# Attention sums through VectorE's 32x32 blocks, a few new places in the second sweep, and a Newton step by scalars

## The chip, the cores and the metric

The kernel runs on one core of one Trainium2 chip. The metric is the device time of one execution in microseconds (us); it is measured as the median of several runs. The kernel's text is a Python program that issues instructions to five engines, each with its own queue in program order: PE (TensorE, matrix products and transposes; PEld is its weight load), DVE (VectorE), ACT (ScalarE), POOL (GpSimd) and SP (SyncE, which here only starts DMAs). ACT's queue starts some DMAs too.

## The reference

One encoder layer over 2048 tokens of width 1024, in float32. The input projection feeds two groups of heads: four heads of bidirectional gated linear attention, and four heads of latent attention with a full softmax. Both pass a SiLU gate, are put side by side, go through one output projection, and end in a residual with LayerNorm:

```python
h = x @ w_in                                    # all projections at once
o_a = rms_norm(o_fwd + o_bwd, norm_g) * silu(gate_a)        # per head, scans over the sequence
...
s = q_nope . k_nope + q_rope . k_rope           # per head, 2048 x 2048
p = softmax(s, axis=-1)
o_b = (p @ v) * silu(gate_b)
...
m = concatenate([o_a, o_b]) @ w_out
t = alpha * x + m
y = (t - mean(t)) * rsqrt(var(t) + 1e-5) * g + b
```

The change touches three small parts of that: the sum that the softmax divides by, the order of work in one sweep, and the `rsqrt` of the last line.

## The kernel before

Products in float32 are made of three matmuls. Each operand is split into a rounded high part (`hi`, a copy by ACT, L364) and a low part (`lo`, a subtraction by DVE or POOL, L370), and `mm3` adds high x high (L418), high x low (L419) and low x high (L420).

**Stages.** A first sweep goes backwards over 16 chunks of 128 tokens (to about 370 us). A second sweep (`sweep_c`, L1145) goes over them in eight steps of two chunks, makes the queries and keys of both groups, and finishes the linear attention (to about 562 us). Then come 16 blocks of softmax attention, each one head and 512 queries, against all 2048 keys in eight pairs of 128 (to about 1125 us), and the output projection by chunks with LayerNorm (the tail).

**Second sweep.** Each chunk's work is a list of named steps (`kvx`, `sqO`, `rml`, ...). A table, `PLACE_C`, gives each step two numbers, for the even and the odd chunk of a pair: the time, in units of one step, at which it is issued. `PLACE_C_LAST` (L284) replaces it in the last step. All steps are sorted by these numbers into one list, and `in_order` ties every engine's instructions into that order, so the tables fix each queue. The steps that the change moves are: `kvx` (L1390, three DVE transposes in 32x32 blocks of the values' high and low part and of the rotary keys, of one chunk; `skv` stores both chunks' from SP's queue), `sqO` (L1507, the squares of the linear attention's output, ACT), and the norm of the compressed queries and keys: `rml` (L431 and L432, a logarithm and an exponential by ACT), `ssm` (L1348, DVE, mean squares), `rmd` (L437 to L440, DVE, the Newton step of that norm). Beside them in the queues stand `xh` (xch, high part of a chunk of x, ACT), `cqTh` and `cqTl` (cqT_h by ACT and cqT_l by DVE, the parts of the compressed queries that PE multiplies at pqr), `krsh` (krs, the keys' high part, ACT), and qrx, qrT (turned rotary queries).

**Attention.** `PLACE` (L82) works in the same way, in units of one pair of keys: eight units are a block, and a block's work is spread over the next two. For each pair, `scores` (L1599 to L1603) writes two PSUM banks, pS, of which there are two pairs; `copy` (L1608) takes them to SBUF by ACT; `smax` (L1621) keeps the running maximum by DVE, reading pS, and so frees it; later `sub` (L1645, DVE) subtracts the maximum, `exp` (L1649, ACT), `hi` and `lo` split the probabilities, `pv` multiplies them with the values. The sum of the probabilities is gathered in two accumulators, four pairs by DVE in PSUM (ap, L1672) and four by POOL in SBUF (acc). `tot` (L1695, L1696, DVE) adds them up to one tile of 128 keys x 512 queries. `tsum` (L1708) turns it by four PE transposes, 128x128 each, into PSUM (sx); `rcp` sums over the keys (L1714, DVE) and takes the reciprocal (L1715); `keep` (L1720, on ACT's DMA queue) stores 512 single values to DRAM. The last block's sum runs in the tail, and the last two blocks' reciprocals go a way of their own, through `turn` (L1726, a PE transpose of 128x4, rt) and `rows` (L1732).

**Tail.** Each chunk's projection (`product`) is followed by `finish` (L2015 to L2027): mean and variance, a pass over two halves of 128x512 with the gain (lng), `rsqrt` of the variance, a second pass (L2026, with lnb), and the store. `rsqrt` is a logarithm and an exponential by ACT (L431, L432) and one Newton step by DVE in `rsqrt_b` (L437 to L440); for `finish` its operands have one element per partition. ACT's, POOL's and SP's order is fixed in the tail; DVE's is left to the scheduler.

## Time and profile before

| | |
|---|---|
| median of 3 runs | 1267.62 us (1267.16 to 1270.45) |
| the profiled execution | 1266.33 us |
| span of its trace | 1264.5 us, granted clock 0.997 |
| instructions | 19632 |
| DMA | 165.61 MB, 131 GB/s on average |

Busy time by stage, us:

| stretch | stage | PE | PEld | DVE | ACT | POOL |
|---|---|---|---|---|---|---|
| 0 to 32 | start | 26.02 | 24.59 | 21.83 | 22.94 | 0.21 |
| 32 to 500 | sweeps | 465.72 | 439.35 | 259.50 | 221.54 | 173.12 |
| 500 to 560 | second sweep's end | 57.49 | 55.05 | 37.06 | 28.28 | 28.10 |
| 560 to 680 | attention begins | 117.80 | 99.29 | 94.14 | 86.17 | 68.01 |
| 1095 to 1130 | attention ends | 35.00 | 29.01 | 16.94 | 3.75 | 18.33 |

How to read what follows: a row of the busy table gives an engine, its busy us, its share of the span and its instructions. A row in order of time gives the start in us, the duration, the engine, the line (L1621 is line 1621 of the kernel), the operation, output<-inputs by the program's names, shapes, and in square brackets the idle time ahead of it with what ended it. A row of a group gives its count, its busy us and the mean ns of one.

### The profile page before, as it was taken

What the parts mean: (1) busy time and instruction counts of PE and PEld (TensorE: products, weight loads), DVE (VectorE), ACT (ScalarE), POOL (GpSimd) and SP (SyncE); (2) the same over time, 40 slices, a digit from 0 to 9 for tenths busy, and PEclk for the clock granted to TensorE, in tenths of its full rate; (3) what the DMA queues carried; (4) which work ended last, traced back from release to release, by engine and by line L of the source; (5) the groups of instructions that cost most, each with busy time, mean ns of one, the idle gap of its engine ahead of it and who ended that gap; (6) DMA issues with size and microseconds to landing.
All of it is one profiled execution on the core that took longest, in us unless ns stands there. A gap on an engine that the chain in (4) does not pass through costs nothing.

```text
span 1264.5 us, 19632 instructions
## 1 busy us (share of the span) xinstructions
PE 1242.3 (98%) x6890; PEld 1094.2 (87%) x6890; DVE 906.0 (72%) x1654; ACT 725.8 (57%) x1149; POOL 721.7 (57%) x443
## 2 busy tenths in 40 slices
PE   8999999999999999999999999999999999999997
PEld 7999999999899999988788888888888888887886
DVE  6635555554565666575988888888888888379998
ACT  7543443444664545445788888788888888411110
POOL 0132323223364555421798888889999999935441
PEclk9999999999999999999999999999999999999999
DMA  8224655556757788868422222202244120477773
GB/s 294 79 81 123 139 143 139 144 135 159 268 179 212 227 244 239 240 183 195 73 37 48 41 43 43 59 9 59 59 94 92 41 43 26 125 205 199 206 199 116
DMA packets 284338, 165.61 MB, mean 131 GB/s; under 512 B 185574, under 2 KB 241774, under 8 KB 284240
## 3 DMA queue, kind: packets, MB, share of 16 engines
q1 hardware_dynamic: 276176, 162.23, 48.2%
q0 software_dynamic: 672, 2.10, 0.4%
q8 instruction: 55, 0.90, 0.4%
q10 hardware_dynamic: 7392, 0.03, 0.3%
q14 instruction: 43, 0.35, 0.1%
HBM read 105.54 MB, written 58.75 MB: 130 GB/s over the span
## 4 chain that ended last, share of the span: by engine, by line
PE 86%; DVE 5%; DMA 3%; issue 2%; SPq 2%; ACT 1%; POOL 1%; DVEq 0%; POOLq 0%; ACTq 0%
PE pz L1266 7%; PE ipm L1335 5%; PE o L418 5%; PE o L419 5%; PE o L420 5%; PE pS L1599 4%; PE pS L1600 4%; PE pS L1602 4%; PE pS L1601 4%; PE pS L1603 4%; PE ipa L418 4%; PE ipa L420 4%; PE ipa L419 4%; PE ipg L420 2%; PE ipg L418 2%; PE ipg L419 2%
## 5 line engine op out<-in xcount | busy, mean ns | idle before, releaser
L370 POOL TENSOR_TENSOR pl<-s,ph 128x1024 fp32r<-128x1024 f32 x128 | 306.6, 2412 | 51.5 <-ACT ph L364 40.9
L1621 DVE TENSOR_TENSOR rm<-pS,rm 128x512 f32<-128x512 f32 x210 | 144.8, 690 | 36.3 <-ACT s L1608 30.7
L1608 ACT ACTIVATE s<-pS 128x1024 f32<-128x1024 f32 x128 | 131.3, 1025 | 60.4 <-PE pS L1603 50.0
L1645 DVE TENSOR_TENSOR s<-s,mb 128x1024 f32<-128x1024 f32 x128 | 151.2, 1213 | 8.9 <-PE mb L1639 8.8
L364 ACT ACTIVATE ph<-s 128x1024 fp32r<-128x1024 f32 x128 | 135.0, 1057 | 16.7 <-PE o L420 16.1
L1649 ACT ACTIVATE s<-s 128x1024 f32<-128x1024 f32 x128 | 131.4, 1049 | 9.4 <-DVE s L1645 9.3
L418 PE MATMUL ipa<-wah,xah 128*128 128x384 f32 (+1 forms) x384 | 128.8, 335 | 5.4 <-ACT wah L364 5.4
L419 PE MATMUL ipa<-wal,xah 128*128 128x384 f32 (+1 forms) x384 | 124.6, 324 | 0.0
L420 PE MATMUL ipa<-wah,xal 128*128 128x384 f32 (+1 forms) x384 | 124.4, 324 | 0.0
L1085 POOL TENSOR_TENSOR Sb<-Sb,Us 64x512 f32<-64x512 f32 x15 | 19.9, 1325 | 170.1 <-DVE Us L1077 161.0
L1599 PE MATMUL pS<-qh,kvT 128*128 128x512 f32 x256 | 102.4, 400 | 0.8 <-DVE rm L1621 0.4
L418 PE MATMUL o<-ph,vh 128*128 128x512 f32 x256 | 101.0, 395 | 0.0
L1600 PE MATMUL pS<-ql,kvT 128*128 128x512 f32 x256 | 99.9, 390 | 0.0
L1602 PE MATMUL pS<-rh,kvT 128*128 128x512 f32 x256 | 99.9, 390 | 0.0
L1601 PE MATMUL pS<-qh,kvT 128*128 128x512 f32 x256 | 99.8, 390 | 0.0
L1603 PE MATMUL pS<-rl,kvT 128*128 128x512 f32 x256 | 99.7, 390 | 0.0
L420 PE MATMUL o<-ph,vl 128*128 128x512 f32 x256 | 99.7, 389 | 0.0
L419 PE MATMUL o<-pl,vh 128*128 128x512 f32 x256 | 99.6, 389 | 0.0
L1672 DVE TENSOR_TENSOR ap<-ap,s 128x512 f32<-128x512 f32 x120 | 83.1, 693 | 2.7 <-ACT s L1649 0.8
L370 POOL TENSOR_TENSOR ol<-of,oh 128x512 fp32r<-128x512 f32 x32 | 43.7, 1365 | 67.8 <-ACT oh L364 62.5
L418 PEld LDWEIGHTS ipa<-wah,xah 128*128 128x128 f32 x384 | 73.1, 190 | 8.3 <-ACT wah L364 5.4
L419 PEld LDWEIGHTS ipa<-wal,xah 128*128 128x128 f32 x384 | 73.1, 190 | 1.0 <-DVE wal L370 0.5
(303 smaller groups left out, 3416.1 us busy)
## 6 DMA issues: line engine op xcount, KB each, us to landing
xcf<-xT_dram SPq DMA_DIRECT2D x16, 512.0 KB, 5.7
xr<-x_dram SPq DMA_DIRECT2D x16, 512.0 KB, 5.9
out_dram<-rr SPq DMA_DIRECT2D x32, 256.0 KB, 2.1
xaf<-xT_dram SPq DMA_DIRECT2D x14, 512.0 KB, 4.1
oib<-oi_s SPq DMA_DIRECT2D x16, 256.0 KB, 4.9
qdb<-qd_s SPq DMA_DIRECT2D x16, 256.0 KB, 3.7
SU<-su_s SPq DMA_DIRECT2D x16, 256.0 KB, 4.8
ub<-u_s SPq DMA_DIRECT2D x16, 256.0 KB, 4.5
```

Of the source, the lines that this page charges most:

```text
L364: return nc.scalar.activation(dst, src, AF.Copy).ins
L370: return e.tensor_tensor(dst, src, hi.bitcast(F32), ALU.subtract).ins
L418: mm(out, ah, bh, start=start, stop=False)
L419: mm(out, ah, bl, start=False, stop=False)
L420: mm(out, al, bh, start=False, stop=stop)
L1599: mm(ps[:, e], kh, qh, start=True, stop=False)
L1600: mm(ps[:, e], kh, ql, start=False, stop=False)
L1601: mm(ps[:, e], kl, qh, start=False, stop=False)
L1602: mm(ps[:, e], kr, rh, start=False, stop=False)
L1603: mm(ps[:, e], kr, rl, start=False, stop=True)
L1621: V.tensor_tensor(d["rm"], src[:, e], d["rm"], ALU.max)
L1645: V.tensor_tensor(s, s, d["mb"][:, None, :].to_broadcast([P, 2, QB]), ALU.subtract)
```

## The change

It has three parts.

1. **Attention sums.** For the first 14 blocks a new step `tpart` follows `tot`: DVE transposes acc within 32x32 blocks (128 x 512 to 128 x 512), so that each partition holds, in each of 16 groups of 32, the values of 32 keys for one query, and sums each group: s16, 128 x 16. `tsum` then is one PE transpose of s16 to 16 x 128, `rcp` sums its four key groups for 16 x 32 queries and takes the reciprocal of 16 x 32, and `keep` stores 16 rows of 32 values. `tsum` gets another place. The last two blocks keep the old way.
2. **Second sweep.** Six numbers in the tables change.
3. **Newton step.** `rsqrt_b` gets a form for operands of one element per partition: three tensor_scalar instructions in which y and u are scalars by pointer, where three tensor_tensor and one tensor_scalar were.

Line numbers of the changed kernel are 1 higher up to L434, 6 higher up to L1703 and 21 higher at the end.

```diff
@@ PLACE @@
-    tsum=12.04,
+    tpart=11.25,
+    tsum=12.44,
@@ PLACE_C @@
-    kvx=(1.12, 1.44),
+    kvx=(1.3, 1.44),
@@ PLACE_C @@
-    sqO=(0.272, 0.988),
+    sqO=(0.272, 0.94),
@@ PLACE_C_LAST @@
-    rml=(0.162, 0.878),
+    rml=(0.187, 0.878),
@@ PLACE_C_LAST @@
-    ssm=(0.103, 0.733),
-    rmd=(0.254, 1.022),
+    ssm=(0.1025, 0.733),
+    rmd=(0.29, 1.022),
@@ rsqrt_b @@
     def rsqrt_b(self, u, y, t, w, r):
         nc = self.nc
+        if u.shape[1] == 1:
+            nc.vector.tensor_scalar(t, y, u, y, ALU.mult, ALU.mult)
+            nc.vector.tensor_scalar(t, t, -0.5, 1.5, ALU.mult, ALU.add)
+            nc.vector.tensor_scalar(r, t, y, None, ALU.mult)
+            return r
         nc.vector.tensor_tensor(t, y, u, ALU.mult)
         nc.vector.tensor_tensor(w, t, y, ALU.mult)
         nc.vector.tensor_scalar(t, w, -0.5, 1.5, ALU.mult, ALU.add)
@@ attention @@
                 p, tag = other if i == nb - 1 else (pX, "x")
                 return p.tile(shape, F32, tag=tag, name=name)
+            def tpart(i):
+                d = stt[i]
+                V.transpose(d["as"][:, 1], d["as"][:, 0])
+                d["s16"] = bs.tile([P, QB // 32], F32, tag="s16", name=f"s16_{i}")
+                V.tensor_reduce(d["s16"], d["as"][:, 1].rearrange("p (b k) -> p b k", k=32), AX.X, ALU.add)
+
             def tsum(i):
                 d = stt[i]
+                if i < nb - 2:
+                    d["x"] = pX.tile([P, 4, P], F32, tag="x", name=f"sx{i}")[0:QB // 32, 0]
+                    nc.tensor.transpose(d["x"], d["s16"], self.ident)
+                    return
                 d["x"] = close(i, [P, 4, P], f"sx{i}", (pA, "ap"))
                 for e in range(4):
                     nc.tensor.transpose(d["x"][:, e], d["as"][:, 0, e * P:(e + 1) * P], self.ident)
@@ attention @@
             def rcp(i):
                 d = stt[i]
-                rc = bs.tile([P, 4], F32, tag="rc", name=f"rc{i}")
+                if i < nb - 2:
+                    rc = d["rc"] = bs.tile([QB // 32, 32], F32, tag="rc", name=f"rc{i}")
+                    V.tensor_reduce(rc, d["x"].rearrange("b (k q) -> b q k", k=4), AX.X, ALU.add)
+                    V.reciprocal(rc, rc)
+                    return
+                rc = bs.tile([P, 4], F32, tag="rc4", name=f"rc{i}")
                 V.tensor_reduce(rc, d["x"], AX.X, ALU.add)
                 V.reciprocal(rc, rc)
                 d["rc"] = rc
             def keep(i):
                 h, b = blocks[i]
-                Ac.dma_start(self.r_s[b][:, h].rearrange("o (e p) -> p (o e)", p=P), stt[i]["rc"])
+                Ac.dma_start(self.r_s[b][:, h].rearrange("o (e q) -> (o e) q", q=32), stt[i]["rc"])
             def turn(i):
@@ attention @@
             put(0.5, nc.sync.dma_start, wv, self.ins["wv"])
             put(8.6, wv_hi)
             put(9.9, self.lo, wv_l, wv, wv_h, "pool")
-            own = (("tot", tot), ("tsum", tsum), ("rcp", rcp), ("keep", keep), ("oh", oh), ("ol", ol), ("y", y), ("yc", yc))
-            own_late = tuple(e for e in own if e[1] is not keep)
+            own = (("tot", tot), ("tpart", tpart), ("tsum", tsum), ("rcp", rcp), ("keep", keep), ("oh", oh), ("ol", ol), ("y", y), ("yc", yc))
+            own_late = tuple(e for e in own if e[1] not in (keep, tpart))
             for i in range(nb):
                 for j in range(NP):
                     t = NP * i + j
```

**The order, first place: DVE in an attention block.** In the middle of the program, from the last addition of block 5's sums to its reciprocal. The numbers after the tags are those of the block (and of the pair): s6_3 is the scores of block 6, pair 3, rm7 block 7's running maximum, mb6 block 6's maximum, ap the accumulator of DVE, ofl the low part of an output. Before:

```order
L1696 TENSOR_TENSOR acc5_8824<-ap5_8690,acc5_8824 128x512
L1621 TENSOR_TENSOR rm7_8917<-pS7_1_8906,rm7_8917 128x512 x2
L1645 TENSOR_TENSOR s6_3_8717<-s6_3_8717,mb6_8893 128x1024
L1621 TENSOR_TENSOR rm7_8917<-pS7_2_8935,rm7_8917 128x512 x2
L1645 TENSOR_TENSOR s6_4_8767<-s6_4_8767,mb6_8893 128x1024
L1645 TENSOR_TENSOR s6_5_8796<-s6_5_8796,mb6_8893 128x1024
L370 TENSOR_TENSOR ofl5_8999<-o5_8756,ofh5_8989 128x512
L1621 TENSOR_TENSOR rm7_8917<-pS7_3_8971,rm7_8917 128x512 x2
L1672 TENSOR_TENSOR ap6_8968<-ap6_8968,s6_0_8624 128x512
L1714 TENSOR_REDUCE rc5_9042<-sx5_8982 128x4
L1715 RECIPROCAL rc5_9042<-rc5_9042 128x4
```

After, from the row behind that addition:

```order
L1627 TENSOR_TENSOR rm7_8917<-pS7_1_8906,rm7_8917 128x512 x2
L1712 STREAM_TRANSPOSE acc5_8824<-acc5_8824 128x512
L1714 TENSOR_REDUCE s16_5_8958<-acc5_8824 128x16
L1651 TENSOR_TENSOR s6_3_8717<-s6_3_8717,mb6_8893 128x1024
L1627 TENSOR_TENSOR rm7_8917<-pS7_2_8935,rm7_8917 128x512 x2
L1651 TENSOR_TENSOR s6_4_8767<-s6_4_8767,mb6_8893 128x1024
L1651 TENSOR_TENSOR s6_5_8796<-s6_5_8796,mb6_8893 128x1024
L371 TENSOR_TENSOR ofl5_8999<-o5_8756,ofh5_8987 128x512
L1627 TENSOR_TENSOR rm7_8917<-pS7_3_8974,rm7_8917 128x512 x2
L1678 TENSOR_TENSOR ap6_8971<-ap6_8971,s6_0_8624 128x512
L1731 TENSOR_REDUCE rc5_9042<-sx5_8991 16x32
L1732 RECIPROCAL rc5_9042<-rc5_9042 16x32
```

The transpose and the sum of acc5 stand ahead of the subtraction for pair 3 of block 6, so that three subtractions, ofl5 and two further pairs of maxima are issued behind them; the rows of rc5 keep their place with smaller shapes. On PE, `L1708 MATMUL sx5_8982<-ident_213,acc5_8824 128x128 x4` became `L1720 MATMUL sx5_8991<-ident_213,s16_5_8958 16x128`, between the same scores, pS7_3 and pS7_4.

**Second place: the second sweep's last step.** Chunks 12 and 14 on DVE, from the keys' turns to the low part of the queries. rm14 is the norm's scale of chunk 14 (ipm14 its input), kvx6 the turned keys and values, Ob14 and ss14 belong to the linear attention's norm. Before, with the third turn first:

```order
L1390 STREAM_TRANSPOSE kvx6_6656<-krs12_6414 128x128
L1446 STREAM_TRANSPOSE qrx12_6660<-qrf12_6542 128x256
L1540 TENSOR_TENSOR krf14_6662<-ipm14_6560,cos_257 128x64
L1544 TENSOR_TENSOR rope1_14_6663<-ipm14_6560,sin_258 128x32 x2
L1512 TENSOR_REDUCE Ob14_6595<-og14_6667 128x4
L1513 TENSOR_SCALAR ss14_6677<-Ob14_6595 128x4
L437 TENSOR_TENSOR rm14_t_6673<-ipm14_6560,ssm14_6637 128x2
L438 TENSOR_TENSOR ipm14_6560<-rm14_t_6673,ipm14_6560 128x2
L439 TENSOR_SCALAR rm14_t_6673<-ipm14_6560 128x2
L440 TENSOR_TENSOR rm14_r_6674<-rm14_t_6673,ipm14_6560 128x2
L370 TENSOR_TENSOR qrT6_6682<-qrx12_6660,qrT6_6682 128x256
L370 TENSOR_TENSOR cqT_l6_6485<-tm13_6669,cqT_h6_6484 128x2x128
```

After:

```order
L1452 STREAM_TRANSPOSE qrx12_6656<-qrf12_6542 128x256
L1546 TENSOR_TENSOR krf14_6658<-ipm14_6560,cos_257 128x64
L1550 TENSOR_TENSOR rope1_14_6659<-ipm14_6560,sin_258 128x32 x2
L1518 TENSOR_REDUCE Ob14_6595<-og14_6663 128x4
L1519 TENSOR_SCALAR ss14_6668<-Ob14_6595 128x4
L371 TENSOR_TENSOR qrT6_6678<-qrx12_6656,qrT6_6678 128x256
L371 TENSOR_TENSOR cqT_l6_6485<-tm13_6665,cqT_h6_6484 128x2x128
L443 TENSOR_TENSOR rm14_t_6674<-ipm14_6560,ssm14_6637 128x2
L444 TENSOR_TENSOR ipm14_6560<-rm14_t_6674,ipm14_6560 128x2
L445 TENSOR_SCALAR rm14_t_6674<-ipm14_6560 128x2
L446 TENSOR_TENSOR rm14_r_6675<-rm14_t_6674,ipm14_6560 128x2
L1396 STREAM_TRANSPOSE kvx6_6696<-vh_3893 128x128
```

The four rows of rm14 and the three turns moved behind qrT6 and cqT_l6. On ACT at the same place (rm14_l is the logarithm, the second ipm14 row the exponential of the norm) before:

```order
L1342 ACTIVATE sqm14_6636,ssm14_6637<-ipm14_6560 128x256
L1343 ACTIVATE sqm14_6636,ssm14_6637<-ipm14_6560 128x128
L1507 ACTIVATE og14_6667<-Ob14_6595 128x512
L431 ACTIVATE rm14_l_6672<-ssm14_6637 128x2
L432 ACTIVATE ipm14_6560<-rm14_l_6672 128x2
L364 ACTIVATE cqT_h6_6484<-tm13_6669 128x2x128
L364 ACTIVATE qrT6_6682<-qrx12_6660 128x256
L364 ACTIVATE vh_3893<-ckv13_6634 128x128
```

After:

```order
L1348 ACTIVATE sqm14_6636,ssm14_6637<-ipm14_6560 128x256
L1349 ACTIVATE sqm14_6636,ssm14_6637<-ipm14_6560 128x128
L1513 ACTIVATE og14_6663<-Ob14_6595 128x512
L365 ACTIVATE cqT_h6_6484<-tm13_6665 128x2x128
L432 ACTIVATE rm14_l_6673<-ssm14_6637 128x2
L433 ACTIVATE ipm14_6560<-rm14_l_6673 128x2
L365 ACTIVATE qrT6_6678<-qrx12_6656 128x256
L365 ACTIVATE vh_3893<-ckv13_6634 128x128
```

cqT_h6 moved ahead of rm14_l and the exponential. In the steady steps ACT's order xch, krs, og became og, xch, krs, and the even chunk's turns stand later on DVE.

**Third place: the tail.** DVE at chunk 5's LayerNorm; u5 is the variance, ln5_y the result of ACT's exponential, rr5 the chunk. Before:

```order
L2023 SCALAR_TENSOR_TENSOR rr5_12192<-rr5_12192,mv5_12198,lng_11712 128x512 x2
L437 TENSOR_TENSOR ln5_t_12205<-ln5_y_12207,u5_12199 128x1
L438 TENSOR_TENSOR ln5_t_12205<-ln5_t_12205,ln5_y_12207 128x1
L439 TENSOR_SCALAR ln5_t_12205<-ln5_t_12205 128x1
L440 TENSOR_TENSOR ln5_r_12206<-ln5_t_12205,ln5_y_12207 128x1
L2026 SCALAR_TENSOR_TENSOR rr5_12192<-rr5_12192,ln5_r_12206,lnb_11713 128x512 x2
```

After:

```order
L2044 SCALAR_TENSOR_TENSOR rr5_12187<-rr5_12187,mv5_12193,lng_11712 128x512 x2
L439 TENSOR_SCALAR ln5_t_12200<-ln5_y_12202,u5_12194 128x1
L440 TENSOR_SCALAR ln5_t_12200<-ln5_t_12200 128x1
L441 TENSOR_SCALAR ln5_r_12201<-ln5_t_12200,ln5_y_12202 128x1
L2047 SCALAR_TENSOR_TENSOR rr5_12187<-rr5_12187,ln5_r_12201,lnb_11713 128x512 x2
```

The place is the same; four instructions became three, of another operation.

## Prediction

> **What bounds the kernel now.** I read the page's busy shares first, then the busy time by stage, then the order of time at the places that the change touches, and last who waited for whom. The page, and of the stages the steady part of attention and the output tail (columns: stretch, its length, then busy us and instructions of PE, PEld, DVE, ACT, POOL, then granted clock, DMA share, GB/s):

> ```profile
> PE 1242.3 (98%) x6890; PEld 1094.2 (87%) x6890; DVE 906.0 (72%) x1654; ACT 725.8 (57%) x1149; POOL 721.7 (57%) x443
> ...
> 680.00:1095.00 415.00, 415.00 (x1906) 343.19 (x1905) 352.31 (x469) 343.58 (x371) 376.94 (x165) 1.00 0.25 54
> ...
> 1130.00:1264.50 134.50, 125.24 (x574) 103.76 (x573) 124.18 (x198) 19.49 (x53) 57.00 (x42) 0.98 0.64 186
> ```

> In attention PE never rests: 415.00 of 415 us. Whatever leaves PE's queue there comes off the span, as long as nobody else becomes late; DVE is at 85% and POOL at 91%. In the tail PE and DVE are both nearly full (125 and 124 of 134.5), so a gain of DVE counts only where PE waits for it.

> **Attention: PE.** For 14 of the 16 blocks four transposes per block become one. PE's sums, a lone transpose of 4 columns (the last two blocks' reciprocals), and the place in one block:

> ```profile
> L1708 PE MATMUL sx<-ident,acc x64: 270/272/273, 639.9 to 1122.7; 128*128 128x128 f32 x64
> ...
> L1726 PE MATMUL rt<-ident,rc x2: 271/272/272, 1144.6 to 1170.3; 128*4 128x128 f32 x2
> ...
> 764.43 0.60 PE L1708 MATMUL sx<-ident,acc 128*128 128x128 f32 x4
> 764.79 0.48 PE L1599 MATMUL pS<-qh,kvT 128*128 128x512 f32 x1
> ```

> Four take 0.60 us and one alone 0.272, so each after the first costs (0.60 - 0.272)/3 = 0.109 us. The lone 4-column transpose also takes 0.272, so I take the new one with 16 columns as one of the old: three times 0.109 are saved, 0.33 us a block, 14 x 0.33 = **4.6 us**. The ends: 0 if another engine takes the time back, 4.6 if none does.

> **Attention: DVE.** It gets a transpose of 128x512 and a sum of 128x512 in SBUF, and its old sum of 128x512 out of PSUM becomes one over 16x128, the reciprocal one over 16x32. Neither new form stands in this trace at this place; the nearest rows (of oT and og in the second sweep, the old sum and reciprocal, and a 128x128 operation out of PSUM):

> ```profile
> L1529 DVE STREAM_TRANSPOSE oT<-og 128x512 f32<-128x512 f32 x16 | 11.4, 712 | 0.5
> ...
> L1512 DVE TENSOR_REDUCE Ob<-og 128x4 f32<-128x512 f32 x16 | 11.1, 693 | 7.3 <-ACT og L1507 7.2
> ...
> L1714 DVE TENSOR_REDUCE rc<-sx 128x4 f32<-128x512 f32 x16 | 10.9, 680 | 0.0
> ...
> L1544 DVE TENSOR_TENSOR rope<-pqr,sin 128x128 f32<-128x128 f32 x32 | 7.6, 279 | 0.0
> ...
> L1715 DVE RECIPROCAL rc<-rc 128x4 f32<-128x4 f32 x16 | 2.9, 179 | 0.6
> ```

> The new pair costs 0.712 + 0.693 = 1.40 us, some 0.05 less where the next instruction starts before the end: 1.35. The new sum lies between 0.279 and 0.680; it reads a quarter of the elements, so I take 0.28; the reciprocal 0.18. Where this goes, in the block from 751 us (DVE, then the first matmul of the scores that overwrite the PSUM pair which the 765.75 row frees):

> ```profile
> 759.84 1.21 DVE L1645 TENSOR_TENSOR s<-s,mb 128x1024 f32<-128x1024 f32 x1
> ...
> 765.75 1.42 DVE L1621 TENSOR_TENSOR rm<-pS,rm 128x512 f32<-128x512 f32 x2 [0.52 <-ACT s L1608]
> 767.08 0.69 DVE L1672 TENSOR_TENSOR ap<-ap,s 128x512 f32<-128x512 f32 x1
> 767.68 0.68 DVE L1714 TENSOR_REDUCE rc<-sx 128x4 f32<-128x512 f32 x1
> ...
> 768.49 1.41 DVE L1672 TENSOR_TENSOR ap<-ap,s 128x512 f32<-128x512 f32 x2
> ...
> 768.55 0.39 PE L1599 MATMUL pS<-qh,kvT 128*128 128x512 f32 x1
> ```

> The pair stands just ahead of the 759.84 row. All behind it on DVE moves by 1.35 us until the running maximum at 765.75, which had 0.52 us of rest: it moves by 0.83 and ends at 765.75 + 1.42 + 0.83 = 768.00. PE asks for that buffer at 768.55, in the changed order 0.33 earlier: 768.22. **0.2 us of room is left, and that is the hinge of this forecast.** Behind it the sum and reciprocal, 0.81 us from 767.68 to 768.49, shrink to about 0.4 and give 0.4 back. The ACT queue's store of the reciprocals waits for them at about the same time as before. So the cover holds and I count DVE's net 0.95 us per block at nothing; without cover each missing 0.1 us costs 1.4 us over 14 blocks.

> **Second sweep.** In the steady steps PE's queue is full, so a reorder can only cost. Squares ahead of x's high part make that copy, and POOL's low part behind it, later by the squares (0.6 us) and a wait of about 0.4. The copy, the low part and PE's first use in one step:

> ```profile
> 514.89 1.05 ACT L364 ACTIVATE xch<-xcf 128x1024 fp32r<-128x1024 f32 x1
> ...
> 516.44 2.42 POOL L370 TENSOR_TENSOR xcl<-xcf,xch 128x1024 fp32r<-128x1024 f32 x1
> ...
> 521.33 0.64 PE L1266 MATMUL pz<-xcl,wzh 128*128 128x256 f32 x4
> ```

> The low part ends at 518.86, 2.5 us ahead of its use: one microsecond later costs nothing. The keys' turns go behind other DVE work while their store keeps its place; the second chunk's turns, which the store waits for too, do not move. The gain is at the last step, the one place where PE waits:

> ```profile
> 552.03 0.38 PE L418 MATMUL pqr<-wqr_h,cqT_h 128*128 128x256 f32 x1 [1.36 <-ACT cqT_h L364]
> ...
> 553.67 0.58 PE L420 MATMUL pqr<-wqr_h,cqT_l 128*128 128x256 f32 x1 [1.15 <-DVE cqT_l L370]
> ...
> 551.50 0.17 ACT L432 ACTIVATE ipm<-rm_l 128x2 f32<-128x2 f32 x1 [1.09 <-DVE rope L1544]
> 551.61 0.37 ACT L364 ACTIVATE cqT_h<-tm 128x256 fp32r<-128x256 f32 x1
> ...
> 550.09 0.30 DVE L1390 STREAM_TRANSPOSE kvx<-vh 128x128 f32<-128x128 f32 x1
> ...
> 550.70 0.40 DVE L1446 STREAM_TRANSPOSE qrx<-qrf 128x256 f32<-128x256 f32 x1
> ...
> 552.12 0.15 DVE L437 TENSOR_TENSOR rm_t<-ipm,ssm 128x2 f32<-128x2 f32 x1
> ...
> 552.77 0.52 DVE L370 TENSOR_TENSOR qrT<-qrx,qrT 128x256 fp32r<-128x256 f32 x1
> 553.21 0.41 DVE L370 TENSOR_TENSOR cqT_l<-tm,cqT_h 128x256 fp32r<-128x256 f32 x1
> ...
> 557.97 0.70 DVE L1503 TENSOR_TENSOR Ob<-Ob,oib 128x512 f32<-128x512 f32 x1 [1.07 <-PE Ob L1500]
> ...
> 562.67 0.39 PE L1266 MATMUL pz<-xch,wzh 128*128 128x256 f32 x1 [0.28 <-DVE og L1523]
> ```

> ACT's high part stood behind an exponential that waits for DVE; it now stands ahead, and the first wait (1.36) goes. What is late next is DVE's low part: the turns (550.09 to 550.70, 0.61 us) and the four norm instructions (552.12 to 552.77, 0.65) now come behind it, so it and PE's second wait end 1.26 earlier. The gain must still pass DVE, whose work ahead of the 557.97 row is unchanged in amount: there it rested 1.07. PE's next wait, at 562.67, is on DVE again, so **1.1 us** comes through. Ends: 0 and 1.36 + 1.15 = 2.5.

> **Output tail.** The only two waits of PE there, and the four Newton instructions with the pass that follows them (min/median/max in ns):

> ```profile
> PE pmb L420 <- POOL ol L370: 0.7, 1, 0.7
> PE rt L1726 <- ACT rt L1732: 0.7, 1, 0.7
> ...
> L437 DVE TENSOR_TENSOR ln_t<-ln_y,u x16: 129/1242/1293, 1124.0 to 1259.2; 128x1 f32<-128x1 f32 x16
> L438 DVE TENSOR_TENSOR ln_t<-ln_t,ln_y x16: 134/726/1218, 1125.6 to 1259.4; 128x1 f32<-128x1 f32 x16
> L439 DVE TENSOR_SCALAR ln_t<-ln_t x16: 130/154/155, 1126.3 to 1259.6; 128x1 f32<-128x1 f32 x16
> L440 DVE TENSOR_TENSOR ln_r<-ln_t,ln_y x16: 138/393/1201, 1127.0 to 1259.8; 128x1 f32<-128x1 f32 x16
> ...
> L2026 DVE SCALAR_TENSOR_TENSOR rr<-rr,ln_r,lnb x32: 706/753/1866, 1127.3 to 1260.7; 128x512 f32<-128x512 f32 x32
> ```

> One element per partition takes 0.13 us or up to 1.29; only the form with one tensor, L439, always stays at 0.15. The long ones fall beside POOL's work. With scalars all three remaining take L439's form, up to 3 us per chunk come free on DVE, and both waits hang on chains through DVE (ACT's norm exponentials, queued ahead of splits and rows). I take the second wait as gone and 0.2 of the first, **0.9 us**: early in the tail DVE's freed time partly turns into waits of L2026, which has two SBUF tensors. The last chunk has nothing beside it: one small instruction less, **0.15 us**. Ends: from 0.7 lost, if L2026 now holds POOL up and the first wait doubles, to 1.4 + 0.15 gained.

> L439 is the row that decides here. [...]

> **Sum.** 4.6 + 1.1 + 0.9 + 0.15 = 6.7 us. The profiled execution took 1266.33 us (span 1264.5 and 1.8 around it): 1259.6. The median shown is 1.3 above it, so I forecast 1267.62 - 6.7 = **1260.9**.

> **Rivals.**
> - *DVE's room of 0.2 us does not hold* (the sum over 16x128 or the pair a few tenths dearer): PE waits at the 768.55 row up to what it saved, and attention gives 0 to 3 us. For it: the small room. Against: 1.35 comes from rows that hardly vary. Time about 1265.5. Chance 0.13.
> - *Slower: POOL locks the new pair out.* A POOL operation begins right ahead of it in every block:

> ```profile
> 759.28 2.42 POOL L370 TENSOR_TENSOR pl<-s,ph 128x1024 fp32r<-128x1024 f32 x1 [2.11 <-ACT ph L364]
> ```

>   If the transpose behaved as L437 does and waited for its end at 761.70, it would start 1.86 us late; less the room of 0.2 and the saved 0.33, 1.3 us a block and 18 us in all: about 1281. The kernel gets slower by over 0.3% from 0.6 us of new waiting per block (14 x (0.6 - 0.33) = 3.8). Against it: oT's 16 runs and og's sums, some beside POOL, all take their means, and both new forms read one tensor. Chance 0.07.
> - *The Newton steps still wait, or the wait only moves to L2026*: the tail gives 0.15 at best or loses 0.7; 1261.8 to 1262.7. Chance 0.10. [...]

> **How the numbers follow.** The forecast has 0.70, with its own range 1258.2 to 1262.6 (terms 4.6, 0 to 2.5, 0 to 1.55, the rest spread between executions). The range of 8 in 10 reaches down to 1257.8 and up to 1266.0, which takes in the tail rival and most of the first. A measurement can tell about 0.3%, 3.8 us, from no change: faster (below 1263.8) is the forecast, the tail rival and few of the first, 0.79; same 0.13; slower 0.08.

> **What would show it.** One sx matmul of 0.27 per block, PE still at 100% in attention and the distance from block to block 0.33 us less; a wait of PE on "rm" at the sixth pair of scores would be the first rival; a transpose of acc over 1 us the second. In the second sweep no wait on cqT_h and cqT_l ready about 1.2 earlier. In the tail Newton rows near 0.15 and no wait of PE on ACT's rt. Wrong would make it above all a room in DVE's queue that I misread.

## The result and the profile after

The changed kernel takes 1260.89 us (median of 6 runs, 1260.13 to 1264.79), the kernel before 1267.71 beside it (6 runs, 1265.96 to 1270.45). The ratio is 0.9951, interval 0.9934 to 0.9968: 6.2 us less, between 4.1 and 8.4. The forecast was 1260.9. The profiled execution of the changed kernel took 1264.79 us, with a span of 1262.9; why it stands 4 us above the median comes out below. So its stages are read one by one, not from its end.

**Attention.** Busy time of the changed kernel in the steady part of attention (columns as before):

```profile
680.00:1090.00 410.00, 410.00 (x1863) 337.46 (x1862) 365.36 (x495) 344.07 (x368) 376.03 (x164) 1.00 0.24 54
```

PE is still at 100%; DVE rose from 85% to 89%. One block, the place that the forecast spoke of, DVE and then PE of the changed kernel:

```profile
760.20 0.70 DVE L1712 STREAM_TRANSPOSE acc<-acc 128x512 f32<-128x512 f32 x1
760.94 0.69 DVE L1714 TENSOR_REDUCE s<-acc 128x16 f32<-128x512 f32 x1
...
766.25 0.68 DVE L371 TENSOR_TENSOR ofl<-o,ofh 128x512 fp32r<-128x512 f32 x1
766.86 1.40 DVE L1627 TENSOR_TENSOR rm<-pS,rm 128x512 f32<-128x512 f32 x2
...
768.77 0.27 DVE L1731 TENSOR_REDUCE rc<-sx 16x32 f32<-16x128 f32 x1
769.07 0.34 DVE L1732 RECIPROCAL rc<-rc 16x32 f32<-16x32 f32 x1
...
764.79 0.27 PE L1720 MATMUL sx<-ident,s 128*16 128x128 f32 x1
764.82 0.48 PE L1605 MATMUL pS<-qh,kvT 128*128 128x512 f32 x1
...
767.21 0.39 PE L419 MATMUL o<-ph,vh 128*128 128x512 f32 x1
...
768.58 0.40 PE L1605 MATMUL pS<-qh,kvT 128*128 128x512 f32 x1
...
795.63 0.27 PE L1720 MATMUL sx<-ident,s 128*16 128x128 f32 x1
```

The kernel before, the same transpose one block later (the row of 764.43 is in the prediction):

```profile
795.56 0.38 PE L1708 MATMUL sx<-ident,acc 128*128 128x128 f32 x2
```

From one sx to the next it was 795.56 - 764.43 = 31.13 us and is 795.63 - 764.79 = 30.84; over the thirteen steps from block to block the distance falls by 0.30, 4.2 us for 14 blocks. The maximum ends at 766.86 + 1.40 = 768.26, the scores that overwrite its PSUM start at 768.58: 0.32 us of room, where the forecast had 0.2. POOL did not lock the transpose out: 0.70 us, in a group of 14 that reaches from 0.700 to 0.703.

**Second sweep, last step.** PE's waits there in the changed kernel, with the first ipm of chunk 13 ahead of them, and then its two waits of the tail (us in total, times, longest):

```profile
538.59 0.37 PE L1341 MATMUL ipm<-wmh,xch 128*128 128x448 f32 x1
...
555.19 0.38 PE L421 MATMUL pqr<-wqr_h,cqT_l 128*128 128x256 f32 x1 [1.32 <-DVE cqT_l L371]
557.77 0.68 PE L1341 MATMUL ipm<-wmh,xcl 128*128 128x448 f32 x2 [1.03 <-POOL xcl L371]
564.25 0.39 PE L1272 MATMUL pz<-xch,wzh 128*128 128x256 f32 x1 [0.44 <-DVE og L1529]
```

```profile
PE pmb L421 <- POOL ol L371: 1.0, 1, 1.0
PE rt L1747 <- ACT rt L1753: 0.8, 1, 0.8
```

The wait for cqT_h is gone and one of 1.03 for xcl is new. The stretch from chunk 13's first ipm to this pz is 564.25 - 538.59 = 25.66 us; I call it the last-step stretch below. In the kernel before it began at

```profile
535.62 0.37 PE L1335 MATMUL ipm<-wmh,xch 128*128 128x448 f32 x1
```

and ended at 562.67: 27.05.

**Tail.** The two waits of PE that were to shrink grew, from 0.7 and 0.7 to 1.0 and 0.8. Busy time from 1126 us on, before and after:

```profile
1126.00:1262.90 136.90, 129.24 (x592) 107.10 (x590) 128.18 (x207) 19.49 (x53) 59.44 (x44) 0.99 0.65 188
```

```profile
1126.00:1262.90 136.90, 126.95 (x581) 104.84 (x579) 102.92 (x186) 19.51 (x53) 63.49 (x43) 0.99 0.66 185
```

DVE is busy 25 us less (128.18 to 102.92), and PE's waits in this trace show nothing of it.

### The profile page after: what moved, and what is told of

It reads as the page before. It is cut to its first block, busy times and chain, and to the rows that moved or that the text cites. A ratio compares the mean times of both kernels' runs of the same rounds, so it can differ in the third digit from the quotient of the medians.

```text
span 1262.9 us, 19554 instructions
## 1 busy us (share of the span) xinstructions
PE 1239.1 (98%) x6848; PEld 1089.6 (86%) x6848; DVE 896.3 (71%) x1666; ACT 729.1 (58%) x1149; POOL 726.5 (58%) x443
## 4 chain that ended last, share of the span: by engine, by line
PE 84%; DVE 4%; DMA 4%; POOL 2%; issue 2%; ACT 2%; SPq 1%; DVEq 0%; POOLq 0%; ACTq 0%
PE pz L1272 7%; PE ipm L1341 5%; PE pS L1605 5%; PE pS L1607 4%; PE pS L1606 4%; PE pS L1608 4%; PE pS L1609 4%; PE o L421 4%; PE o L419 4%; PE o L420 4%; PE ipa L419 4%; PE ipa L421 4%; PE ipa L420 4%; PE ipg L421 2%; PE ipg L419 2%
## 5 line engine op out<-in xcount | busy, mean ns | idle before, releaser
L420 PE MATMUL ipa<-wal,xah 128*128 128x384 f32 (+1 forms) x384 | 125.0, 325 | 0.0
L1608 PE MATMUL pS<-rh,kvT 128*128 128x512 f32 x256 | 99.8, 390 | 0.0
L420 PE MATMUL o<-pl,vh 128*128 128x512 f32 x256 | 99.7, 389 | 0.0
L1272 PE MATMUL pz<-xch,wzh 128*128 128x256 f32 x256 | 73.4, 290 | 1.4 <-DVE og L1529 1.3
```

The source lines that it names most:

```text
L420: mm(out, ah, bl, start=False, stop=False)
L1272: self.nc.tensor.matmul(s["pz"][:, h], self.Wz[k][w][:, h * P:(h + 1) * P], x2(x, k), start=(k == 0 and p == 0), stop=stop.get(h) == (k, p))
L1608: mm(ps[:, e], kr, rh, start=False, stop=False)
```

## Experiments

All ratios are to the kernel before, run beside on the same chip. The theory on trial is the prediction's sum: 4.6 for the sums, 1.1 for the second sweep, 1.05 for the Newton step. The rivals were that one part brings it all, that DVE gives time back, and, after the first traces, that in the second sweep it is the granted clock and not the waits.

**The parts alone** (`e1_sums`, `e2_sweep`, `e3_newton`: the kernel before with one part of the diff; `e4_no_newton`: the changed kernel without the form for one element).

> Only the attention sums are changed (tables and Newton step as before). The forecast gave this part 4.6 us: 1267.7 - 4.6 = 1263.1, ratio 0.9964; the distance of 31.12 us between blocks on PE falls by 0.30 to 0.33, PE stays without a wait. Rival (DVE's room does not hold, it gives the time back): ratio 0.998 to 1.000, with waits of PE on the running maximum. Rival (the time of the changed kernel came from elsewhere): ratio 1.000.

> Only the six places in the second sweep are changed. The forecast gave 1.1 us: 1266.6, ratio 0.9991, no wait of PE on cqT_h in the last step. Second theory, from the trace of the changed kernel: the wait on cqT_h (1.4) goes, the one on cqT_l stays at about 1.2, and a new one of about 1.0 on POOL's xcl appears, so 0.3 us is left: 1267.4, ratio 0.9998. Either is within what the time can tell; the waits in the trace decide.

> Only the Newton step of the LayerNorm is changed. The forecast gave 0.9 + 0.15 us: 1266.6, ratio 0.9992, no wait of PE on ACT's rt and a shorter one on POOL's ol. Rival, now the likelier after the trace of the changed kernel: DVE is busy 25 us less in the tail and PE's two waits stay at 0.7 each or grow by up to 0.9 in all: 1267.5 to 1268.6, ratio 1.000 to 1.0007.

> The changed kernel with the old Newton step. The forecast: 1.05 us slower than the changed kernel, 1261.9, ratio to before 0.9955. Rival: the Newton step by scalars gains nothing or loses up to 0.8, so this is at 1260.1 to 1260.9, ratio 0.994 to 0.9947.

| run | median us | ratio | interval | us |
|---|---|---|---|---|
| e1_sums | 1261.85 | 0.9958 | 0.9945 to 0.9970 | -5.3 |
| e2_sweep | 1266.59 | 0.9988 | 0.9979 to 0.9997 | -1.5 |
| e3_newton | 1266.56 | 0.9992 | 0.9982 to 1.0002 | -1.0 |
| e4_no_newton | 1261.53 | 0.9958 | 0.9943 to 0.9973 | -5.3 |

The sums bring most. The second sweep gains more than the 0.3 of the second theory; the last-step stretch is 25.67 and 25.68 in e2 and e4, and 27.81 and 27.83 in e1 and e3, which keep the old order. (My expectations name its ends wrongly: it runs from chunk 13's first ipm to the last step's first pz. The values 27.81 and 27.83 are with a half clock, of which more below.) The Newton step's interval reaches both sides.

**Where the second sweep's gain is.** PE waited 1.36 + 1.15 + 0.28 = 2.79 us in the last-step stretch of the trace before, and 1.32 + 1.03 + 0.44 = 2.79 in that of the changed kernel: waits alone don't make it 1.4 us shorter. The granted clock, the share of its full clock that PE is given, differs. Kernel before, the stretch behind the two waits, then e1_sums in steps of 3.41 us, the old order too (after the length come PE's busy us; PEclk is the third number from the end):

```profile
553.37:556.78 3.41, 3.10 (x10) 2.87 (x11) 3.24 (x13) 0.51 (x2) 2.69 (x3) 0.50 0.74 217
```

```profile
548.57:551.98 3.41, 2.06 (x12) 1.51 (x10) 3.31 (x16) 1.52 (x6) 0.00 (x0) 1.00 1.04 348
551.98:555.39 3.41, 1.73 (x10) 1.14 (x8) 3.17 (x14) 0.91 (x5) 3.21 (x3) 1.00 0.61 189
555.39:558.81 3.42, 3.32 (x14) 3.24 (x15) 1.59 (x5) 0.00 (x0) 1.05 (x3) 0.50 0.37 101
```

For 3.41 us after a stretch in which PE was busy 1.73 of 3.41, the clock is 0.50. All five traces with the old order and unfilled waits (before, e1, e3, e12 and e5 below) have it there. To test whether PE's idleness makes it, and what it costs, PE gets useless matmuls in the very waits. The first try put them one chunk too early, at chunk 12 (in e9_fill_wait below it is 13); the 8 stand ahead of the matmul that waits for cqT_l:

```diff
+        def fill(n, first):
+            for _ in range(n if d["c"] == 12 else 0):
+                mm(pq[:, 256:], self.wqr_h[:, 0, :P], self.wqr_h[:, 0], start=first, stop=first)
+        fill(11, True)
...
+            if ct == 0:
+                fill(8, False)
```

> The kernel before, with 19 more matmuls (128x256, results unused) on PE in the second sweep's last step: 11 in the wait for cqT_h (1.36 us) and 8 in the wait for cqT_l (1.15 us), of 0.12 us each, so that PE is busy there and still waits for the same things. Theory of the clock: the half granted clock of 3.41 us that follows these two waits in all three traces with the old order is caused by PE's idleness, and it is most of what the new order gained there. It then goes away, the stretch from chunk 15's ipm to the last pz falls from 27.8 to about 26.1 us, and the time by 1.5 to 1.7: ratio 0.9987. Rival (the waits themselves are the cost, the clock's dip is chance or a mere consequence): the stretch stays at 27.0 to 27.8, the dip stays in the trace, ratio 1.000.

`e5_fill_old`: 1268.3 us, ratio 1.0013 (1.0004 to 1.0023). The matmuls ran at 540.35 to 542.8 us, where PE had no wait, and by estimate cost 19 x 0.119 = 2.3 us there (0.119 from one to the next); both waits and the half clock stayed (6.83 us of it this time). So it tells nothing of the waits, but something of the price of PE's time where its queue is full: 0.5 to 2.9 us more by the interval, for 2.3 us of matmuls.

> The changed kernel with the same kind of matmuls: 11 in the wait of about 1.3 us for cqT_l in the last step, 5 ahead of chunk 3's turn near 409 us, where two waits stand close together. Theory of the clock: no half clock between 20 and 1250 us in the trace, slow executions (above 1262.5) disappear, median 1259.8 to 1260.6. Rival: the fill changes nothing or costs its 0.12 us per matmul, 1260.9 to 1262.8, with the same spread as the changed kernel (1260.1 to 1264.8).

`e6_fill_new`, the changed kernel with the same mistake (11 matmuls near 542 us) and 5 ahead of chunk 3's turn near 408: 1261.88 us, ratio 0.9963 (0.9950 to 0.9976), 1.0 us above the changed kernel's median: about the price of the 11 (11 x 0.119 = 1.3 us). Its executions still spread from 1260.59 to 1263.75, against the expectation, although the trace of the slowest of them holds no half clock between 20 and 1250 us. So the half clock is not the only thing that spreads them.

> As e5_fill_old, but the 19 matmuls stand in chunk 13's pqr, whose two waits they are to fill; in e5_fill_old they stood one chunk early, where PE does not wait. Theory of the clock: no half clock behind 550 us in the trace; ipm of chunk 15 to the last pz takes about 26.1 us instead of 27.0 to 27.8; time 1.0 to 1.7 below the kernel before, ratio 0.9987 to 0.9992. Rival: dip and stretch stay, ratio 1.000.

`e9_fill_wait`: 1265.67 us, ratio 0.9986 (0.9977 to 0.9995): 1.8 us faster, between 0.6 and 2.9, by work that nobody uses. PE's rows and the windows:

```profile
535.86 0.37 PE L1335 MATMUL ipm<-wmh,xch 128*128 128x448 f32 x1
...
553.92 0.39 PE L1446 MATMUL pqr<-wqr_h,cqT_l 128*128 128x256 f32 x1 [0.20 <-DVE cqT_l L370]
556.10 0.67 PE L1335 MATMUL ipm<-wmh,xcl 128*128 128x448 f32 x2 [0.62 <-POOL xcl L370]
562.40 0.39 PE L1266 MATMUL pz<-xch,wzh 128*128 128x256 f32 x1 [0.28 <-DVE og L1534]
```

```profile
549.00:552.40 3.40, 3.35 (x23) 2.96 (x22) 3.33 (x16) 1.50 (x7) 0.00 (x0) 1.00 1.01 335
552.40:555.80 3.40, 2.88 (x18) 2.27 (x18) 3.12 (x16) 1.10 (x6) 3.00 (x3) 1.00 0.64 211
555.80:559.20 3.40, 3.10 (x25) 3.08 (x26) 2.77 (x9) 0.60 (x1) 1.25 (x3) 1.00 0.43 111
```

The order is the old one, the matmul behind the wait for cqT_l starts where it did (553.92 - 535.86 = 18.06; before, 553.67 - 535.62 = 18.05), and the clock stays at 1.00. The stretch is 26.54 us, against 27.05 to 27.83 with the half clock. So the clock cost 0.5 to 1.3 us in the old order, and the better order brings another 0.9 (26.54 to 25.66). The new order is not immune: in the trace of e8_last_two below, which has the same tables, a half clock follows the same two waits, and the stretch takes 561.65 - 535.03 = 26.62 us in place of 25.66.

**Is the new wait on xcl worth removing?** `e10_xl` moves POOL's low part of chunk 15 ahead (`xl=(-0.244, 0.3)` to `(-0.244, 0.22)`); it also has the next experiment's edit.

> The changed kernel with the sums of all blocks in the new way, and POOL's low part of chunk 15's x moved ahead of vl of chunk 13, which stands waiting for ACT for 4.4 us. If the wait on xcl is what took the place of the wait on cqT_h, it goes (1.03 us), the stretch from chunk 15's ipm to the last pz falls from 25.68 to about 24.7, and with one wait left there is no half clock there: time 0.7 to 1.3 below e8_last_two, ratio to before 0.9933 to 0.9938. Rival (the next wait, on og, grows instead): within 0.4 of it, 0.9943.

1259.71 us, ratio 0.9945 (0.9927 to 0.9962). PE's rows:

```profile
535.50 0.37 PE L1341 MATMUL ipm<-wmh,xch 128*128 128x448 f32 x1
...
552.11 0.39 PE L421 MATMUL pqr<-wqr_h,cqT_l 128*128 128x256 f32 x1 [1.33 <-DVE cqT_l L371]
...
561.18 0.39 PE L1272 MATMUL pz<-xch,wzh 128*128 128x256 f32 x1 [0.90 <-DVE og L1529]
```

The wait on xcl is gone and the one on DVE's og has doubled, 0.44 to 0.90, with 0.2 on og elsewhere: the stretch is 25.68 us, as without the edit. The rival holds. DVE ends this stretch, and any wait ahead of it is only its shadow.

**The room in DVE's queue.** `e7_twice` is the changed kernel with one line more:

```diff
                 V.transpose(d["as"][:, 1], d["as"][:, 0])
+                V.transpose(d["as"][:, 1], d["as"][:, 0])
```

> The changed kernel with DVE's transpose of the sums issued twice in each of 14 blocks: DVE gets 0.65 us more per block, PE nothing. The room that the trace of the changed kernel shows between the fourth pair's maximum and the scores that overwrite its PSUM is 0.32 us (the forecast had 0.2). Theory of the hinge: PE waits 0.33 us per block for the maximum, blocks take 31.15 instead of 30.82, the time rises by 4.6: 1265.5. Rival (DVE's time is hidden by other slack): 1260.9, blocks unchanged.

1271.15 us, ratio 1.0035 (1.0023 to 1.0047): about 10 us above the changed kernel, twice what I expected. One block:

```profile
765.03 0.27 PE L1721 MATMUL sx<-ident,s 128*16 128x128 f32 x1
765.22 0.47 PE L1605 MATMUL pS<-qh,kvT 128*128 128x512 f32 x1
...
767.98 0.50 PE L419 MATMUL o<-ph,vh 128*128 128x512 f32 x1 [0.24 <-DVE ofl L371]
...
796.56 0.27 PE L1721 MATMUL sx<-ident,s 128*16 128x128 f32 x1
```

```profile
PE o L419 <- DVE ofl L371: 3.3, 14, 0.3
```

A block takes 796.56 - 765.03 = 31.53 us, 0.69 more than 30.84: next to nothing of the added 0.70 is hidden. PE is held up at two places that I had not named: at the first matmul of the next output, which waits until ofl has read the old one out of PSUM (in the changed kernel ofl ends at 766.25 + 0.68 = 766.93, the matmul starts at 767.21: 0.28 of room), and at the scores behind sx (0.19 from one to the other, 0.03 in the changed kernel), which overwrite what the third pair's maximum reads. The two waits add up, 0.15 and about 0.5; the second is more than 0.70 less the room there, in part because the matmul behind it is slow too (0.50 in place of 0.39, the next one 0.34 behind it in place of 0.23). So the pair of 1.39 us used up most of the cover: what remains is some 0.3 us at two places, ofl and the fourth pair's maximum, and 0.74 at the third pair's (762.67 + 1.41 = 764.08 to 764.82).

**The last two blocks.** `e8_last_two` gives them the new way too (the condition goes in tsum and rcp, and with it the old form):

```diff
-                if i < nb - 2:
...
-            own_late = tuple(e for e in own if e[1] not in (keep, tpart))
+            own_late = own
...
-                    for f in {4: (tot, oh, ol), 5: (tsum, rcp), 7: (turn, y, rows, yc)}.get(c, ()):
+                    for f in {4: (tot, tpart, oh, ol), 5: (tsum, rcp), 7: (keep, y, yc)}.get(c, ()):
...
-                    if c == 6:
-                        turn(nb - 2)
-                        rows(nb - 2)
```

> The changed kernel with the new way of the sums in the last two blocks too: one transpose each instead of four, and the reciprocals stored as in the others, so the two transposes rt and their copies and stores by ACT and SP go. By the forecast's terms 2 x 0.30 of PE and two rt transposes with the wait of about 0.8 for ACT's copy: 1.5 to 1.9 less, 1259.2. Rival (the tail from 1142 to 1170 us is set by DVE's and POOL's chains and the loads, and PE's freed time becomes another wait): within 0.5 of the changed kernel.

1259.12 us (1258.23 to 1259.50), ratio 0.9943 (0.9932 to 0.9955). The two ratios, 0.9951 and 0.9943, lie inside each other's interval, so the time alone doesn't tell it from the changed kernel. In the trace, from the last block's maximum to the last matmul, PE takes 194.25 us (start of the first mx to start of the last matmul), against 195.26 to 197.46 in the eleven traces that keep the two rt transposes; of the other two without them e11 takes 194.93, and e10, with a half clock in the tail, 198.23. So it points to the 1.5 that was expected and doesn't prove it.

**All together.** `e11_all` is e10_xl with matmuls in PE's waits, as in e9 and e6:

> As e10_xl, with 5 matmuls of 0.12 us in PE's wait near 409 us (ahead of chunk 3's turn) and 10 in the wait for cqT_l in the last step. Theory of the clock: no half clock between 20 and 1240 us in any execution, so the spread between executions is below 1.5 us and the median 0 to 0.6 below e10_xl, ratio 0.993. Rival: the matmuls cost up to their 1.8 us, ratio 0.9945 or more.

1259.99 us (1258.71 to 1260.37), ratio 0.9938 (0.9925 to 0.9951). No half clock in the trace between 20 and 1250 us, and its six executions lie within 1.7 us, those of e10_xl (1258.51 to 1263.85) within 5.3; the median isn't below e10's by more than chance. It beats the kernel before clearly; against the changed kernel and e8_last_two the intervals overlap. The narrow spread proves little, as e8's five executions lie within 1.3 us without any matmuls in the waits.

**Newton's room.** `e12_newton_more` is the kernel before, with

```diff
...
+        if 4 <= c <= 6:
+            t, r = (sm.tile([P, 1], F32, tag=f"more_{n}", name=f"more{c}_{n}") for n in "tr")
+            kern.rsqrt_b(args[0], args[1], t, t, r)
...
```

> The kernel before, with the old Newton step done a second time, into scratch, for chunks 4 to 6 of the tail, where PE's waits of the tail stand: some 6 us more of DVE there. The forecast took PE's two waits (0.7 each) to hang on DVE's chains, so that DVE's time counts: then they grow, PE's stretch from the last block's maximum to its last matmul rises beyond the 195.4 to 197.4 us of the traces with the old step, and the time by 1 to 6: ratio 1.001 to 1.005. Rival: DVE has that much room in the tail, and neither taking Newton time away nor adding it moves PE by more than chance: ratio 0.9995 to 1.0005.

1267.96 us, ratio 1.0005 (0.9996 to 1.0014). Waits of PE:

```profile
PE pmb L420 <- POOL ol L370: 1.1, 1, 1.1
PE rt L1726 <- ACT rt L1732: 0.7, 1, 0.7
```

The one wait is 1.1 instead of 0.7, the other unchanged, and PE's stretch in the tail 197.46 us, the end of the range. The rival fits better; a loss of up to 1.8 us isn't excluded. The test is weaker than it was meant to be: the twelve added instructions took 7.7 us, but the step's own 64 took 30.6 in place of 35.8, so DVE got only 2.5 us more of it.

## Why the prediction was right, and where not

**Sum.** 1260.9 was forecast, 1260.89 measured. That they agree to 0.01 us is luck: the difference to the kernel before is known to about 2 us, and the kernel before stood at 1267.71 this time. The -6.2 us comes from parts that are right in kind and partly off in size: 4.2 in place of 4.6, 1.4 to 2.1 in place of 1.1 (less where the new order gets its half clock too, as in e8), and 0 to 1 in place of 1.05.

**Attention, PE: right, a little dear.** Three transposes of 0.109 were to go, 0.33 a block; 0.30 went. One sx of 16 columns now takes 0.03 us of PE's queue (764.79 to 764.82) where four took 0.35, but the matmuls of the scores and the outputs take 0.03 more per block than before (18.42 and 10.99 against 18.40 and 10.98); why, the trace doesn't say. 14 x 0.30 = 4.2; e1's interval, 3.8 to 7.0 us, holds it. The first rival (DVE's room fails) and the second (POOL locks the pair out) did not happen. (The second's 1281 takes the saved 0.33 off twice; from its own 1.3 us a block it would have been about 1284.)

**Attention, DVE: the cover held, with a place missed.** The pair took 0.70 + 0.685 (forecast 0.71 + 0.69), the sum over 16x128 0.27 (0.28), the reciprocal 0.34 (0.18). "0.2 us of room is left" was 0.32 at the place named, but ofl and the next output stood as close, 0.28, and e7 shows that PE pays for 0.70 more with 0.69. The hinge was read right in size and not complete: I had followed the maximum's buffers and not the output's.

**Second sweep: the chain right, the clock missed.** The first wait went, and the matmul behind the second stands 1.45 us earlier (555.19 - 538.59 = 16.60 against 18.05; forecast 1.26). That DVE's og sets what comes through is shown by e10. The failed step is the sum's "1.1 us comes through": it took the trace's times as if PE ran at full clock. A half clock of 3.41 us lay in that very stretch, caused by the two waits: it goes when they are filled (e9), and it came in only one of six traces with the new order, where the waits stand further apart. e9 has 0.5 to 1.3 us for it and 0.9 for the order. The sum also left out POOL: the wait of 1.03 for xcl was not foreseen, though e10 shows that nothing hangs on it. And the last step was not "the one place where PE waits": in the kernel before, PE waits 0.48 for cq and 0.88 for og near 409 us too, which is where the half clock of the profiled execution comes from.

**Steady steps: right.** From the first pqr to chunk 13 PE takes 165.78 us in e1 (old tables) and 165.53 and 165.60 in e2 and e4 (new). Over all the traces without a half clock or added matmuls there it is 165.8 to 166.5 with the old tables (five) and 165.5 to 166.7 with the new (five): no loss.

**Tail: the instructions right, the gain not shown.** DVE's rows from 1100 us on, before and after (count, busy us, mean ns, idle time ahead with its cause):

```profile
L2026 DVE SCALAR_TENSOR_TENSOR rr<-rr,ln_r,lnb 128x512 f32<-128x512 f32 x32 | 36.3, 1179 | 0.4
L437 DVE TENSOR_TENSOR ln_t<-ln_y,u 128x1 f32<-128x1 f32 x16 | 13.1, 824 | 1.6 <-ACT ln_y L432 1.6
```

```profile
L2047 DVE SCALAR_TENSOR_TENSOR rr<-rr,ln_r,lnb 128x512 f32<-128x512 f32 x32 | 38.4, 1239 | 0.4
L2032 DVE SCALAR_TENSOR_TENSOR rr<-xr,po 128x512 f32<-128x512 f32 x16 | 10.5, 682 | 28.1 <-POOL ol L371 20.0 <-DMA xr<-x_dram 4.1 <-PE pmb L421 2.2
...
L439 DVE TENSOR_SCALAR ln_t<-ln_y,u 128x1 f32<-128x1 f32 x16 | 4.3, 268 | 1.9 <-ACT ln_y L433 1.9
```

As forecast, no scalar form ever waits (none takes more than 0.275 us), and the second pass with two SBUF tensors takes a little longer (1.18 to 1.24 us). The Newton rows fell from 35.8 us to 10.1. It was right, too, that PE's wait for rt hangs on DVE: ACT's copy of rt stands behind a logarithm and an exponential that wait for DVE's variance u, in both traces. DVE's rows ahead of that variance, before:

```profile
1160.43 1.25 DVE L437 TENSOR_TENSOR ln_t<-ln_y,u 128x1 f32<-128x1 f32 x1
1161.71 1.21 DVE L438 TENSOR_TENSOR ln_t<-ln_t,ln_y 128x1 f32<-128x1 f32 x1
...
1163.15 1.13 DVE L440 TENSOR_TENSOR ln_r<-ln_t,ln_y 128x1 f32<-128x1 f32 x1
1164.32 2.53 DVE L2026 SCALAR_TENSOR_TENSOR rr<-rr,ln_r,lnb 128x512 f32<-128x512 f32 x2
1166.77 0.68 DVE L2011 SCALAR_TENSOR_TENSOR rr<-xr,pmb 128x512 f32<-128x512 f32 x1
```

After:

```profile
1156.98 2.74 DVE L2047 SCALAR_TENSOR_TENSOR rr<-rr,ln_r,lnb 128x512 f32<-128x512 f32 x2
1165.21 0.69 DVE L2032 SCALAR_TENSOR_TENSOR rr<-xr,pmb 128x512 f32<-128x512 f32 x1 [5.49 <-DMA xr<-x_dram]
```

The failed step is "I take the second wait as gone and 0.2 of the first": it left out what else the residual (rr<-xr,pmb) needs. In the kernel before, long Newton rows stand right ahead of it; in the changed kernel DVE has done with them early and idles 5.49 us for the load of x (xr), which SP issues at 1158.56 and which takes 6.46 us to land. In the kernel before SP issues it at 1160.72, and the loads of x around it take 5.9 and 6.5 us, so by estimate it landed close to 1166.77, where the residual begins: the two paths were about equally long. All seven traces with the new step have this idle time (4.3 to 5.5 us); the seven with the old have 0 to 1.5. The wait for rt went in two of the four traces with the new step that have an rt (e3, e6) and stayed at 0.85 and 0.67 in the others (after, e7).

POOL took part of the gain back. Its products with the gate, before and after:

```profile
L1944 POOL TENSOR_TENSOR of<-of,gr 128x512 f32<-128x512 f32 x22 | 29.4, 1338 | 2.3 <-DMA of<-ob_s 1.5
L1965 POOL TENSOR_TENSOR of<-of,gr 128x512 f32<-128x512 f32 x22 | 35.7, 1623 | 3.4 <-DMA of<-ob_s 2.5
```

Their mean is 1.33 to 1.36 us in all seven traces with the old step and 1.60 to 1.62 in all seven with the new, where DVE's second pass runs beside them (1156.98 to 1159.72 beside POOL's 1157.43 to 1160.86). In traces that keep rt, PE's stretch in the tail is 195.35 to 197.46 with the old step (seven) and 195.26 to 197.07 with the new (four): no difference beyond chance. The end chain lost 0.02 us, not 0.15: from the first Newton row to the second pass it takes 1258.45 - 1257.71 = 0.74 us, before 1260.01 - 1259.25 = 0.76, as three scalar forms take 0.27 + 0.15 + 0.21 and the four old ones beside nothing 0.15 + 0.16 + 0.15 + 0.16. What e3 has, -1.0 between -2.3 and +0.3, stays open: the Newton step brings 0 to 1 us, and no run settles it. The third rival, at 0.10, came nearer in size, but not by its reason: the Newton rows don't wait any more, and the second pass grew by only 2 us. None of the 48 scalar rows waited (0.259 to 0.275, 0.134 to 0.155 and 0.195 to 0.215 us), 35 of them beside POOL's work; of the old 64, the rows with two tensors took up to 1.29 us there.

**The changed kernel's profiled execution** has a half clock of its own near 412 us, where a wait of 0.83 for cq and one of 0.88 for og stand close together:

```profile
409.03:412.44 3.41, 1.77 (x13) 1.53 (x14) 3.20 (x16) 2.02 (x8) 2.81 (x2) 1.00 1.05 329
412.44:415.85 3.41, 3.41 (x19) 3.41 (x18) 3.31 (x13) 1.83 (x8) 2.92 (x4) 0.50 0.71 174
```

The steady steps take 168.09 us there against 165.5 to 166.7, and PE comes to the second sweep 1.4 us later than in the trace before (first pqr at 370.49 against 369.11): together some 3 to 4 us.

## What to carry to other kernels

Where an engine is full, as PE is in attention, its work can be priced by the instruction (0.33 us a block forecast, 0.30 measured), and the question is only which other engine still has room: look for every buffer that the engine's queue frees, not only the nearest. Where PE waits, look at the granted clock behind the wait before a price is put on it: two short waits side by side can cost more than their sum (here 1.36 and 1.15 us, and 0.5 to 1.3 more for the 3.41 us at half clock behind them), and filling them with useless matmuls (1.8 us in e9_fill_wait), or moving them apart (the half clock in one trace of six in place of five of five), can be a gain of its own. And before busy time saved on an engine is counted, look for the other inputs of the instruction that ends its chain: 25 us of DVE here moved nothing that can be measured, because a load of x arrived no earlier.
